# Whole float32 matmuls in the decode and the retention, instead of split fp32r parts

## The chip, the cores and the metric

The kernel runs on one core of one Trainium2 chip. The metric is device time in microseconds, as the median of the timed runs. The profile is of one execution. Engines are named as the profile names them: PE (TensorE's matmuls), PEld (its weight loads), DVE (VectorE), ACT (ScalarE), POOL (GpSimd) and SP (SyncE, whose queue issues every DMA here).

## What is computed

One step of a layer with three gated branches, for a prompt of 2048 tokens and for 8 sequences that are decoded, 16 new tokens each. One projection of the normed input feeds all branches; each branch's output is gated, projected, merged and projected again. Cut to the parts that the change touches:

```python
def fox_attend(q, c_q, q_pos, k, v, c_k):            # 8 heads x 64; decode: 16 queries, 2048 cached keys + 16 new
    s = einsum('bqhd,bkhd->bhqk', q, k) * 64 ** -0.5
    s = s + c_q[..., :, None] - c_k[..., None, :]    # cumulated log forget gates (axes moved)
    p = softmax(where(k_pos <= q_pos, s, -inf))
    return einsum('bhqk,bkhd->bqhd', p, v)

def retention_block(q, k, v, s, log_g):              # 4 heads, qk 128, v 256, state s 128 x 256
    inter = einsum('blhk,bhkv->blhv', q, s) * dec_q
    intra = einsum('bhlm,bmhv->blhv', einsum('blhk,bmhk->bhlm', q, k) * dmask, v)
    s_new = exp(log_g * L) * s + einsum('blhk,blhv,hl->bhkv', k, v, dec_k)
    return inter + intra, s_new

def memory_attend(q, mk, mv):                        # 4 heads x 128; decode: 16 queries, 256 cached memory tokens
    p = softmax(einsum('bthd,bmhd->bhtm', q, mk) * 128 ** -0.5)
    return einsum('bhtm,bmhd->bthd', p, mv)
```

## The kernel before

All multiplications keep close to float32 precision by splitting: a float32 operand x becomes a high part h (x cast to fp32r, on ACT) and a low part l = x - h (on DVE or POOL), and a product is three fp32r matmuls: h by h, h by l, l by h (`mm3` at L225, `mm3r` at L230; `split` at L200). The work runs in three stages.

The *projection* (to 1683 us) makes all of q, k, v and the gates and leaves them in DRAM; the FoX and memory queries and keys are stored there already split (qtH, qtL, ktH, ktL, mqH, mqL), the retention's q, k, v are stored whole.

Then *two lanes* are woven by hand-set costs (`weave`, L1007; the lanes at L1771 and L1792), so that the program order of their steps alternates; each engine then runs its own instructions in order. The right lane is the retention and then FoX's prompt attention. The left lane is the forget gates' sums, the prompt's memory attention (`mem_prompt`), the decode's memory attention (`decode_mem`), FoX's decode (`decode_fox`) and the first output block. The last stage is the other *output blocks*.

*Retention* (L1109). Sixteen units of 128 tokens and one for the 8 decoded sequences (`sample`), each started one step after the last. A unit loads q, k, v, transposes q and k (8 transposes), splits q (qh, ql), k (knh, knl) and v (vh, vl) in `ret_parts`, multiplies whole float32 scores of 128 columns in `ret_scores` (L1062) and splits the masked scores (smh, sml). Its outputs are 24 fp32r matmuls of 256 columns into `ry` (L1138) and its new state 12 into `rm` (L1146); the state is split for the next unit. Later steps normalise, gate, transpose and store (`ret_store`). `sample` runs sixteen steps, for each sequence and pair of heads: load a state, split it, mask query and key parts for the sequence (L1215, L1218), multiply 6 and 6 fp32r matmuls, add the decayed state and store it.

*FoX decode* (L1405). For each of 8 sequences: the queries of all heads stand as four 128 x 128 blocks (`qblk`), high and low. For each of four chunks of 512 cached keys, the keys come as rows (tile dkt), and for each group of 128 features four transposes (L1500) bring them to feature-major, `split` makes dkh and dkl, and `mm3r` multiplies 3 x 512 columns; a selector matmul (L1505) adds the forget sums. After the softmax the probabilities are transposed and split (dpr), the values (dvt) are split on POOL into dvh and dvl (L1542, L1543), and the values are multiplied as 64 fp32r matmuls of 256 columns (L1548): the stationary operand holds the high and the low probabilities of 64 rows side by side, and `sumid` adds the two halves at the end (L1564).

*Memory decode* (L1627) does the same with 256 memory tokens: 16 transposes (L1659), `split` into mkh and mkl, 12 matmuls of 256 columns, values cast and split (mvh, mvl), 4 matmuls of 512.

Of the kernel before, what the change touches and what calls it, by code (L numbers as in the profile page):

```python
# [72 lines left out]
def body(ctx: ExitStack, tc: tile.TileContext, a, o, stop=99):  # L73
# [106 lines left out]
    def f32(t):  # L180
        return t.bitcast(F32)
# [853 lines left out]
    def ret_parts(rw, q, k, v):  # L1035

        qt = rw.tile([P, 512], F32, name="qt")
        kt = rw.tile([P, 512], F32, name="kt")
        qh = rw.tile([P, 512], F32R, name="qh")
        ql = rw.tile([P, 512], F32R, name="ql")  # L1040
# [5 lines left out]
        S.copy(qh, qt)  # L1046
        G.tensor_tensor(ql, qt, f32(qh), ALU.subtract)
        knh = rw.tile([P, 512], F32R, name="knh")
        knl = rw.tile([P, 512], F32R, name="knl")
        S.copy(knh, k)  # L1050
        G.tensor_tensor(knl, k, f32(knh), ALU.subtract)
        vh = rw.tile([P, 1024], F32R, name="vh")
        vl = rw.tile([P, 1024], F32R, name="vl")
        S.copy(vh, v)
        G.tensor_tensor(vl, v, f32(vh), ALU.subtract)
        return qt, kt, qh, ql, knh, knl, vh, vl

    def ret_scores(rw, qt, kt, mask, nm="sm"):
# [4 lines left out]
        sm = rw.tile([P, 512], F32, name=nm, bufs=1)  # L1063
        V.tensor_tensor(sm, sc, mask, ALU.mult)
        smh = rw.tile([P, 512], F32R, name="smh")
        sml = rw.tile([P, 512], F32R, name="sml")
        S.copy(smh, sm)
        G.tensor_tensor(sml, sm, f32(smh), ALU.subtract)
        return smh, sml
# [21 lines left out]
    def ret_gate(rw, ob, i, sa, nb, g, nm="y"):  # L1091

        y = rw.tile([P, 1024], F32, name=nm)
# [15 lines left out]
    def retention(rp, rw):  # L1109
        NG, OB = 4, 5  # L1110
        cur = [None, None, None]
# [3 lines left out]
        def unit(t):  # L1115
# [3 lines left out]
            qt, kt, qh, ql, knh, knl, vh, vl = ret_parts(rw, q, k, v)  # L1119
            yield  # L1120
            smh, sml = ret_scores(rw, qt, kt, mask)
            yield
            so, soh, sol = cur
            ob = rw.tile([P, 4, 256], F32, name="ob", bufs=OB)
            for h2 in range(2):
                op = pry()

                prods = []
                for rnd in range(4):
                    for i in range(2):  # L1130
                        h = 2 * h2 + i
                        c = slice(h * P, (h + 1) * P)
# [725 lines left out]
```

## Time and profile before

| | us |
|---|---|
| median of the three timed runs | 3410.53 |
| fastest, slowest | 3404.25, 3414.77 |
| the profiled execution's own time | 3406.5 |
| its span, first to last instruction | 3404.7 |

| share of the span | PE | PEld | DVE | ACT | POOL |
|---|---|---|---|---|---|
| busy | 94% | 88% | 67% | 51% | 36% |

A matmul's record is longer than the time after which the next one starts, so a busy PE is not a full PE; the starts of matmuls in a row show what one costs. A group of instructions is named by its line, engine, operation and tiles (written <- read); its idle time is that of the engine just before the group's instructions, with what ended it. A stretch is a window of time from the span's start.

### The profile page before, as it was taken

To read this page: it belongs to the slowest core of one execution; us is meant where nothing else is said; L and a number is where in the kernel's file an instruction comes from. 1 tells how busy PE (TensorE), PEld (TensorE's weight loads), DVE (VectorE), ACT (ScalarE), POOL (GpSimd) and SP (SyncE) were. 2 spreads that over 40 slices of the span, in tenths; PEclk is the share of its full clock that TensorE was granted. 3 is DMA by queue.
4 is the path that set the end of the run, shared out by engine and by line. 5 is a ranking of instruction groups with operands and counts; after the bars stand their busy time and mean duration, and the time that the engine had idled before them with its cause. 6 is when DMAs were issued, how large, how long until landed. Compare 5 with 4: busy or idle time off the path is not lost. (4 is left out here: it accounts for less than half of the span.)

```text
span 3404.7 us, 60285 instructions
## 1 busy us (share of the span) xinstructions
PE 3195.5 (94%) x22299; PEld 2997.7 (88%) x22299; DVE 2271.3 (67%) x3732; ACT 1743.5 (51%) x3404; POOL 1217.7 (36%) x1122
## 2 busy tenths in 40 slices
PE   6999999999999999999878888999999988999999
PEld 5998999999999999999868766888887888888899
DVE  7677676665565666565588877887777886545444
ACT  4453444555344555445468755767776764223222
POOL 4436443110220010220176443777776764100000
PEclk8999999999999999999999987999999999999999
DMA  4776566567557667667567765455654457676665
GB/s 166 230 246 201 180 209 198 190 211 253 168 167 215 203 212 244 205 192 220 192 198 230 243 195 162 153 157 162 179 179 148 129 151 224 184 223 204 191 188 166
DMA packets 628219, 660.94 MB, mean 194 GB/s; under 512 B 46060, under 2 KB 549252, under 8 KB 627860
## 3 DMA queue, kind: packets, MB, share of 16 engines
q1 hardware_dynamic: 627924, 657.08, 62.5%
q8 instruction: 176, 2.88, 0.3%
q14 instruction: 119, 0.97, 0.1%
HBM read 477.52 MB, written 179.41 MB: 193 GB/s over the span
## 5 line engine op out<-in xcount | busy, mean ns | idle before, releaser
L400 DVE TENSOR_TENSOR wl<-wr,wh 128x1024 fp32r<-128x1024 f32 (+1 forms) x386 | 568.4, 1476 | 286.9 <-ACT wh L399 282.1
L399 ACT CAST wh<-wr 128x1024 fp32r<-128x1024 f32 (+1 forms) x386 | 404.6, 1050 | 309.9 <-PE b L451 128.0
L449 PE MATMUL a<-wh,ho 128*128 128x256 f32 (+1 forms) x1432 | 408.4, 286 | 18.1 <-ACT gz L707 11.3
L450 PE MATMUL a<-wl,ho 128*128 128x256 f32 (+1 forms) x1432 | 406.3, 284 | 5.8 <-DVE wl L400 5.8
L451 PE MATMUL a<-wh,ho 128*128 128x256 f32 (+1 forms) x1432 | 407.0, 284 | 1.0 <-DVE ho L276 1.0
L428 POOL TENSOR_TENSOR wr<-wr 128x1024 f32<-128x1024 f32 (+1 forms) x72 | 202.1, 2806 | 270.0 <-DMA wr<-in_w_in 235.0
L451 PE MATMUL b<-wh,ho 128*128 128x256 f32 (+1 forms) x1032 | 290.5, 282 | 5.4 <-DVE ho L276 5.4
L449 PE MATMUL b<-wh,ho 128*128 128x256 f32 (+1 forms) x1032 | 291.3, 283 | 4.0 <-ACT wh L399 2.3
L221 ACT CAST wh<-wraw 128x1024 fp32r<-128x1024 f32 x120 | 123.3, 1049 | 334.9 <-DMA wraw<-in_w_p 131.4
L449 PEld LDWEIGHTS a<-wh,ho 128*128 128x128 f32 x1432 | 273.4, 191 | 22.1 <-ACT gz L707 13.7
L450 PE MATMUL b<-wl,ho 128*128 128x256 f32 (+1 forms) x1032 | 290.4, 282 | 0.5 <-DVE wl L400 0.5
L450 PEld LDWEIGHTS a<-wl,ho 128*128 128x128 f32 x1432 | 273.7, 191 | 6.3 <-DVE wl L400 6.3
L451 PEld LDWEIGHTS a<-wh,ho 128*128 128x128 f32 x1432 | 273.7, 191 | 1.5 <-DVE ho L276 1.5
L449 PE MATMUL a<-ho,wh 128*128 128x384 f32 (+1 forms) x768 | 252.6, 329 | 1.6 <-ACT gz L707 1.6
L450 PE MATMUL a<-ho,wh 128*128 128x384 f32 (+1 forms) x768 | 252.9, 329 | 0.0
L451 PE MATMUL a<-ho,wl 128*128 128x384 f32 (+1 forms) x768 | 252.1, 329 | 0.0
L460 ACT COPY kp<-a 128x256 f32<-128x256 f32 (+3 forms) x384 | 153.3, 404 | 183.5 <-PE a L451 182.0
L1334 ACT ACTIVATE pt<-sc,f_mx 128x512 f32<-128x512 f32 (+2 forms) x320 | 201.5, 631 | 73.2 <-DVE f_mx L1333 48.4
L1338 POOL TENSOR_SCALAR pt<-pt,f_f,f_nm 128x512 f32<-128x512 f32 (+3 forms) x288 | 208.6, 740 | 82.2 <-DVE f_nm L1262 28.9
L1333 DVE TENSOR_REDUCE f_mx<-sc 128x1 f32<-128x512 f32 (+2 forms) x320 | 192.6, 604 | 39.4 <-PE sc L1327 21.7
L205 DVE TENSOR_TENSOR pl<-tp,ph 128x512 fp32r<-128x512 f32 (+2 forms) x352 | 193.5, 562 | 34.6 <-ACT ph L202 33.0
L1745 POOL TENSOR_TENSOR gm<-gm,gm 128x512 f32<-128x512 f32 (+2 forms) x40 | 45.6, 1139 | 447.4 <-DVE gm L1743 447.3
(437 smaller groups left out, 9901.0 us busy)
## 6 DMA issues: line engine op xcount, KB each, us to landing
wr<-in_w_in SPq DMA_DIRECT2D x170, 512.0 KB
wraw<-in_w_p SPq DMA_DIRECT2D x80, 512.0 KB
dkt<-in_cache_fox_k SPq DMA_DIRECT2D x64, 512.0 KB
dvt<-in_cache_fox_v SPq DMA_DIRECT2D x64, 512.0 KB
wr<-sum_gl SPq DMA_DIRECT2D x48, 512.0 KB
wraw<-in_w_out SPq DMA_DIRECT2D x40, 512.0 KB
gtd<-gz SPq DMA_DIRECT2D x96, 192.0 KB
gt<-gtd SPq DMA_DIRECT2D x24, 768.0 KB
```

Source lines behind the costliest of these rows:

```text
L205: V.tensor_tensor(l, src, f32(h), ALU.subtract)
L221: S.copy(whv[:, i * hc:(i + 1) * hc], rv)
L399: S.copy(h, t)
L400: eng.tensor_tensor(l, t, f32(h), ALU.subtract)
L428: G.tensor_tensor(out, x, y, op)
L449: T.matmul(out, lh(c), rh(c), start=first and c == 0, stop=False, skip_group_check=True)
L450: T.matmul(out, lh(c), rl(c), start=False, stop=False, skip_group_check=True)
L451: T.matmul(out, ll(c), rh(c), start=False, stop=last and c == 3, skip_group_check=True)
L460: S.copy(t[nm], t["a"])
L1333: V.tensor_reduce(nmx[:, j, ci:ci + 1], sc[:, :w], AX.X, ALU.max, negate=True)
L1334: S.activation(pt[:, :w], sc[:, :w], AF.Exp, bias=nmx[:, j, ci:ci + 1], accum_out=l[:, j, ci:ci + 1])
L1338: G.tensor_scalar(pt, pt, fb, 0.5 if r is None else r[:, j:j + 1], ALU.mult, ALU.mult)
```

## The change

The FoX decode, the memory decode and the retention multiply whole float32 operands, one float32 matmul for each three (or, for the decode's values, two half-wide pairs) of fp32r. The splits of q, k, v, scores, states, cached keys and cached values there go; the FoX and memory queries and new keys, which DRAM holds as two parts, are added together once (qw, kw). The cached keys of both attentions are handed to the kernel feature-major, so their transposes go as well. The masks of `sample` move from DVE to POOL, and the decay of the state goes into DVE's sum. The retention's order of state and output is swapped, and its tiles get more buffers. Nothing else is touched: FoX's prompt attention, the prompt's memory attention, the projection and the output blocks keep the split.

The diff, cut:

```diff
@@ ret_load, ret_turn (was ret_parts), ret_scores
-        q = rp.tile([P, 512], F32, name="rq")
-        k = rp.tile([P, 512], F32, name="rk")
-        v = rp.tile([P, 1024], F32, name="rv")
+        q = rp.tile([P, 512], F32, name="rq", bufs=2)
+        k = rp.tile([P, 512], F32, name="rk", bufs=4)
+        v = rp.tile([P, 1024], F32, name="rv", bufs=4)
...
-        S.copy(qh, qt)
-        G.tensor_tensor(ql, qt, f32(qh), ALU.subtract)
-        S.copy(knh, k)
-        G.tensor_tensor(knl, k, f32(knh), ALU.subtract)
-        S.copy(vh, v)
-        G.tensor_tensor(vl, v, f32(vh), ALU.subtract)
+        return qt, kt
...
-        S.copy(smh, sm)
-        G.tensor_tensor(sml, sm, f32(smh), ALU.subtract)
@@ retention, unit
-                for n, (dst, l, r) in enumerate(prods):
-                    T.matmul(dst, l, r, start=n == 0, stop=n == len(prods) - 1)
...
-                    mm3(up[:, (h % 2) * 256:(h % 2 + 1) * 256], knh[:, c], knl[:, c], vh[:, vc], vl[:, vc], True, True)
+                    T.matmul(up[:, i * 256:(i + 1) * 256], k[:, h * P:(h + 1) * P], v[:, h * 256:(h + 1) * 256], start=True, stop=True)
...
-                split(snh, snl, sn)
+                    T.matmul(op[:, i * 256:(i + 1) * 256], sm[:, h * P:(h + 1) * P], v[:, h * 256:(h + 1) * 256],
+                             start=i == 0, stop=t == 0 and i == 1)
+                        T.matmul(op[:, i * 256:(i + 1) * 256], qt[:, h * P:(h + 1) * P], so[:, h], start=False, stop=i == 1)
...
             y = ret_gate(rw, ob, j, *scales[t // NG], g)
             yield
+            yield
             ret_store(rw, y, t)
@@ retention, sample
-                    split(s0h, s0l, s0)
-                    G.tensor_tensor(s0, s0, gpb[:, hs], ALU.mult)
-                        V.tensor_copy(z[:, :, bs], f32(src).rearrange("p (h l) -> p h l", h=4)[:, hs, bs])
-                        V.tensor_scalar(z, f32(src)[:, h2 * 256:(h2 + 1) * 256], kc[:, K_BM + b:K_BM + b + 1], None, ALU.mult)
+                    G.tensor_copy(zb[:, :, bs], qt.rearrange("p (h l) -> p h l", h=4)[:, hs, bs])
+                    G.tensor_scalar(zk, k[:, h2 * 256:(h2 + 1) * 256], kc[:, K_BM + b:K_BM + b + 1], 1.0, ALU.mult, ALU.mult)
...
-                        mm3r(op[:, oc], zb[0][:, i], zb[1][:, i], s0h[:, i], s0l[:, i], False, b == NB - 1 and i == 1)
-                        mm3(up[:, oc], zk[:, 0, c], zk[:, 1, c], vh[:, vc], vl[:, vc], True, True)
-                    V.tensor_tensor(sn, up.rearrange("p (h v) -> p h v", h=2), s0, ALU.add)
+                        T.matmul(op[:, oc], zb[:, i], s0[:, i], start=False, stop=b == NB - 1 and i == 1)
+                        T.matmul(up[:, oc], zk[:, i * P:(i + 1) * P], v[:, h * 256:(h + 1) * 256], start=True, stop=True)
+                        V.scalar_tensor_tensor(sn[:, i], s0[:, i], kc[:, K_GP + 4 + h:K_GP + 5 + h], up[:, i * 256:(i + 1) * 256], ALU.mult, ALU.add)
@@ decode_fox
+        for w, (h, l) in ((qw, qs), (kw, ks)):
+            V.tensor_tensor(w, f32(h), f32(l), ALU.add)
...
-            kv = a["cache_fox_k"][b].rearrange("(p j) c -> p j c", p=P)
+            kv = a["cache_fox_k"][b].rearrange("g p k -> p g k")
...
-                        kt = dw.tile([P, 2, 512], F32, name="dkt", bufs=3)
-                        dma(kt, kv[:, 4 * ci + 2 * j:4 * ci + 2 * j + 2])
-                            T.transpose(p[:, j * P:(j + 1) * P], kts[j][:, g4 * P:(g4 + 1) * P], ident)
-                        split(kh, kl, p)
-                        mm3r(sc, qb[0][:, g4], qb[1][:, g4], kh, kl, g4 == 0, False)
+                        kt = dw.tile([P, 2, 512], F32, name="dkt", bufs=4)
+                        dma(kt, kv[:, 2 * g2:2 * g2 + 2, ci * 512:(ci + 1) * 512])
+                            T.matmul(sc, qb[:, 2 * g2 + g], kt[:, g], start=g2 == 0 and g == 0, stop=False)
...
-                split(prv[:, :, 0], prv[:, :, 1], p[:rows, :n * P].rearrange("p (a c) -> p a c", c=64))
+                S.copy(pr[:rows, :n], p[:rows, :n * P].rearrange("p (j c) -> p j c", c=P))
...
-                            vt = dw.tile([P, 2, 512], F32, name="dvt")
+                            vt = dw.tile([P, 2, 512], F32, name="dvt", bufs=4)
-                                G.tensor_scalar(vh[:, i], vt[:, i], 1.0, 1.0, ALU.mult, ALU.mult)
-                                G.tensor_tensor(vl[:, i], vt[:, i], f32(vh)[:, i], ALU.subtract)
-                                T.matmul(ov[:, c], lt, part[:, j % 2, c], start=ci == 0 and j == 0 and a2 == 0 and part is vh, stop=False)
+                        T.matmul(ov, pr[:, j], vt[:, j % 2], start=ci == 0 and j == 0, stop=False)
@@ decode_mem
-                        T.transpose(p[:, (2 * hh + m) * P:(2 * hh + m + 1) * P], kt[:, m, h * P:(h + 1) * P], ident)
-                split(kh, kl, p)
-                mm3r(sc[:64, :256], qb[0][:, h], qb[1][:, h], kh[:, c], kl[:, c], h == 0, h == 3)
+                T.matmul(sc[:64, :256], qb[:, h], kt[:, h], start=h == 0, stop=h == 3)
...
-                T.matmul(ov, lt, vh[:, m], start=m == 0, stop=False)
-                T.matmul(ov, lt, vl[:, m], start=False, stop=m == 1)
+                T.matmul(ov[:64], pr[:, m], vt[:, m], start=m == 0, stop=m == 1)
@@ _layout
+        "cache_fox_k": i["cache_fox_k"].reshape(NB, P, 16, 4, P).transpose(0, 3, 4, 2, 1).reshape(NB, 4, P, PAST), ...
+        "cache_mem_k": i["cache_mem_k"].reshape(NB, NMEM, 4, P).transpose(0, 2, 3, 1), ...
```

## Rows read from the trace of the kernel before

**Rows 1.** Windows by stage: us, busy time (instructions) of each engine, clock, DMA share.
```profile
1683.00:1757.00 74.00, 46.38 (x295) 39.58 (x294) 54.48 (x107) 40.36 (x76) 47.80 (x30) 0.82 0.69 209
1757.00:1902.00 145.00, 125.05 (x1000) 119.38 (x999) 122.26 (x282) 124.46 (x270) 98.68 (x86) 0.98 0.75 231
1902.00:2003.00 101.00, 83.50 (x588) 75.12 (x588) 84.70 (x233) 56.80 (x130) 47.61 (x64) 0.92 0.82 255
2003.00:2083.00 80.00, 54.54 (x255) 41.11 (x254) 50.55 (x158) 34.15 (x90) 29.69 (x42) 0.67 0.55 157
2083.00:2765.00 682.00, 652.86 (x4551) 563.17 (x4549) 535.63 (x1159) 475.67 (x1259) 492.87 (x648) 0.98 0.50 153
2765.00:3405.00 640.00, 617.00 (x3799) 557.84 (x3798) 350.37 (x485) 204.18 (x276) 99.98 (x81) 0.99 0.65 197
```

**Rows 2.** Timeline of PE: start us, us, line, tiles, shape, count; matmuls in a row.
```profile
1499.73 0.28 PE L449 MATMUL a<-wh,ho 128*128 128x256 f32 x1
...
1505.06 0.31 PE L449 MATMUL a<-ho,wh 128*128 128x320 f32 x1
...
2939.70 0.40 PE L226 MATMUL mr<-ih,wh 128*128 128x512 f32 x1
...
2945.79 0.39 PE L228 MATMUL mm<-ih,wl 128*128 128x512 f32 x1
...
2001.67 0.27 PE L1659 MATMUL tp<-kc,mkt 128*128 128x128 f32 x1
...
2007.89 1.04 PE L1659 MATMUL tp<-kc,mkt 128*128 128x128 f32 x8
...
1686.43 1.16 PE L1062 MATMUL rm<-qt,kt 128*128 128x128 f32 x8 [1.74 <-ACT kt L1045]
...
2223.79 1.00 PE L1564 MATMUL tp<-sumid,dos 128*128 128x64 f32 x8
```

**Rows 3.** Groups of PE by form, 2083 to 2765: count, busy, mean ns, idle before.
```profile
L1326 PE MATMUL sc<-ka,qa 128*128 128x512 f32 x195 | 88.3, 453 | 4.3 <-ACT pt L1334 4.1
...
L234 PE MATMUL ys<-dkl,qb 128*128 128x512 f32 x127 | 57.4, 452 | 7.3 <-DVE dkl L205 4.3 <-DVE f_nm L1257 3.0
L232 PE MATMUL ys<-dkh,qb 128*128 128x512 f32 x127 | 57.0, 449 | 4.6 <-ACT dkh L202 4.6
L1548 PE MATMUL ym<-dvh,dpr 128*128 128x256 f32 x256 | 52.4, 286 | 2.1 <-DVE dpr L205 2.1
```

**Rows 4.** Groups by form of ACT, POOL and DVE, 1683 to 2050, around the retention.
```profile
L1054 ACT CAST vh<-rv 128x1024 fp32r<-128x1024 f32 x17 | 18.0, 1059 | 9.2 <-DMA rv<-rvd 8.3 <-PE ry L1138 0.9
L202 ACT CAST sth<-st 128x1024 fp32r<-128x1024 f32 x15 | 16.0, 1065 | 7.4 <-DVE st L1152 7.4
...
L1055 POOL TENSOR_TENSOR vl<-rv,vh 128x1024 fp32r<-128x1024 f32 x17 | 44.8, 2635 | 25.7 <-ACT vh L1054 25.4
...
L1047 POOL TENSOR_TENSOR ql<-qt,qh 128x512 fp32r<-128x512 f32 x17 | 29.5, 1733 | 8.2 <-ACT qh L1046 5.0 <-issue 3.0 <-POOL vl L1055 0.2
...
L205 DVE TENSOR_TENSOR stl<-st,sth 128x1024 fp32r<-128x1024 f32 x15 | 23.5, 1566 | 0.6 <-ACT sth L202 0.6
...
L1218 DVE TENSOR_SCALAR kt<-knl,kc 128x256 fp32r<-128x256 f32 x16 | 10.3, 642 | 0.0
```

**Rows 5.** Groups by form of ACT, DVE and POOL, 2083 to 2765: the decode's splits.
```profile
L202 ACT CAST dkh<-tp 128x512 fp32r<-128x512 f32 x126 | 71.9, 589 | 62.1 <-PE tp L1500 60.0 <-PE ov L1380 0.7
...
L205 DVE TENSOR_TENSOR dkl<-tp,dkh 128x512 fp32r<-128x512 f32 x126 | 84.2, 685 | 43.0 <-ACT dkh L202 42.5
...
L1543 POOL TENSOR_TENSOR dvl<-dvt,dvh 128x512 fp32r<-128x512 f32 x124 | 156.8, 1285 | 0.5
```

**Rows 6.** Timeline of POOL and ACT, 1690 to 1760: start us, us, operation, idle before.
```profile
1710.52 5.41 POOL L1047 TENSOR_TENSOR ql<-qt,qh 128x512 fp32r<-128x512 f32 x1
...
1721.68 6.18 POOL L1055 TENSOR_TENSOR vl<-rv,vh 128x1024 fp32r<-128x1024 f32 x1
...
1732.59 0.59 ACT L1139 COPY ob<-ry 128x512 f32<-128x512 f32 x1 [8.54 <-PE ry L1138]
```

More of the change, by code (lines that the diff above doesn't have):

```diff
@@ L1153, in unit @@
                 else:
-                    S.copy(sn[:, hs], u)
+                    S.copy(sn[:, 2 * h2:2 * h2 + 2], u)
             if t == 15:
                 dma(o["ret_state_p"].rearrange("h k v -> k h v"), sn)
-            else:
-                snh = rw.tile([P, 4, 256], F32R, name="sth")
-                snl = rw.tile([P, 4, 256], F32R, name="stl")
-                split(snh, snl, sn)
-                cur[:] = [sn, snh, snl]
+            cur[0] = sn
+            for h2 in range(2):
+                op = pry()
+                for i in range(2):
+                    h = 2 * h2 + i
+                    T.matmul(op[:, i * 256:(i + 1) * 256], sm[:, h * P:(h + 1) * P], v[:, h * 256:(h + 1) * 256],
+                             start=i == 0, stop=t == 0 and i == 1)
+                if t:
+                    for i in range(2):
+                        h = 2 * h2 + i
+                        T.matmul(op[:, i * 256:(i + 1) * 256], qt[:, h * P:(h + 1) * P], so[:, h], start=False, stop=i == 1)
+                S.copy(ob[:, 2 * h2:2 * h2 + 2], op.rearrange("p (h v) -> p h v", h=2))
             j = t % NG
@@ L1509, in unit @@
                     for g4 in range(4):
[L1510 removed]
+                        T.matmul(sc[:, :16], qb[:, g4], kw[:, g4, bs], start=g4 == 0, stop=False)
                     T.matmul(sc[:, :16], selr[:16], cnT[:, bs], start=False, stop=False)
@@ L1551, in unit @@
                     dma(f32(vn), f32(vhl)[SEQ + b * TS:SEQ + (b + 1) * TS])
-                    for a2 in range(2):
-                        c = slice(a2 * 256, (a2 + 1) * 256)
-                        lt = pr[:16, 0, a2].rearrange("p r c -> p (r c)")
-                        T.matmul(ov[:, c], lt, vn[:, 4 * a2:4 * a2 + 4, 0:64], start=False, stop=False)
-                        T.matmul(ov[:, c], lt, vn[:, 4 * a2:4 * a2 + 4, 64:128], start=False, stop=a2 == 1)
+                    vw = dw.tile([16, 8, 64], F32, name="dvw", bufs=1)
+                    V.tensor_tensor(vw, f32(vn)[:, :, 0:64], f32(vn)[:, :, 64:128], ALU.add)
+                    T.matmul(ov, pr[:16, 0], vw.rearrange("p h d -> p (h d)"), start=False, stop=True)
                     os = dw.tile([P, 512], F32, name="dos", bufs=1)
@@ L1698, in unit @@
             for h in range(4):
-                T.matmul(p[:, h * 64:(h + 1) * 64], os[:, h * P:(h + 1) * P], sumid, start=True, stop=True)
+                T.transpose(p[:, h * 64:(h + 1) * 64], os[:, h * P:(h + 1) * P], ident[:64, :64])
             for h in range(4):
```

184 lines of the change are left out of this document (58 added, 126 removed).

## The prediction

> **What bounds the kernel now.** I read the stretches first [rows 1]: a table of five engines by stage. The projection ends at 1683 us and the last output blocks begin at about 2765; the diff touches neither. Between them lie four stretches: the start of the retention (1683 to 1757), its steady part beside the prompt's memory attention (to 1902), its sample beside the decode's memory attention (to 2003), a changeover (to 2083), and the long one (to 2765), the FoX prompt attention beside the FoX decode. The busy share of TensorE is a poor guide there, since a matmul's record reaches well past the start of the next. So I next took the time from start to start of matmuls that run back to back [rows 2]: 45 steps of 256 fp32r columns take 5.33 us, 0.118 each; 26 steps of 512 columns take 6.09, 0.234 each; eight transposes take 1.04 with 0.27 for the last, as a single one shows, so 0.11 each. A whole float32 matmul has two records: eight records of 128 columns take 1.16, so 0.126 a record, and eight of 64 columns take 1.00, so 0.104.
>
> With these steps I weigh each stretch. The steady part has 1000 records of forms that all lie near 0.117: 117 of 145 us, 81%. By the same count the start fills 35 of 74 (47%), the sample 70 of 101 (70%), the changeover 34 of 80 (43%, at a mean clock of 0.67 of full speed). In the long stretch 803 of 4551 records are 512 wide (195 of each score pass, 127 of each of the decode's three key passes, 32 selector rows [rows 3]): 188 us; the other 3748 at 0.113 in the mean are 423: 611 of 682, 90%. So TensorE bounds the long stretch, and the retention has several engines near the same level: in its steady part DVE is busy 84%, ACT 86%, POOL 68% and the DMA engines 75% [rows 1].
>
> **What the change does to TensorE.** No row shows a float32 matmul wider than 128 columns, and this price carries the sum. A 128-column record at 0.126 is longer than a 256-column fp32r matmul (0.118) and than the 64-column record (0.104), so it isn't the weight load that sets it; 0.126 fits two passes of 128 columns at the rate of fp32r. Taken on: two records of 0.234 for 256 columns (0.47), two of 0.47 for 512 (0.94). The ends: four times the 128-column matmul, 1.01; and, if the step from 64 to 128 columns (0.023) goes on as it is, 0.53. I take 0.94, nearest to the fp32r rows of the same widths.
>
> FoX decode, per batch row. Now: 64 key transposes (7.0), 48 score matmuls of 512 (11.2), 64 value matmuls of 256 (7.6), and 2.6 for new keys, new values and the final sums: 28.3. After: 16 scores of 512 (15.0), 16 values of 512 (15.0), and 2.6: 32.6. The difference of 4.3, eight times, is **+34 us of TensorE work** in the long stretch.
>
> Retention, per block of 128: 36 fp32r matmuls of 256 (4.25) become 12 float32 ones (5.6): +1.4, and +21 over 16 blocks. Sample: 192 and 12 fp32r matmuls (24.1) become 64 and 4 (32.0): +8. Memory decode: 16 transposes, 12 matmuls of 256, 4 of 512 and the sums (5.0) become 4 of 256, 2 of 512 and 4 transposes (4.2): -6 over eight rows. Together +23 up to 2083.
>
> **What it takes off the other engines.** In the retention the splits go [rows 4]: ACT loses vh and the state's cast (1.06 each) and three casts of half that width, some 4 us a block; POOL loses vl (2.64) and three like ql, 6.5 a block or more; DVE loses the state's low part, 1.6. In the sample POOL takes over DVE's masking of keys and queries: 256 and 32 columns a step, at most half and a sixteenth of ql's 1.7 us, about 1, and it loses the state's decay, 512 columns. In the long stretch ACT loses the key casts, DVE their low parts, POOL the values' low parts [rows 5], 72, 84 and 157 of 476, 536 and 493 us busy, and POOL the values' high parts too.
>
> *Start, 1683 to 1757: -10 (-18 to 0).* POOL's chain stands in the way here: one ql takes 5.41 us beside a mean of 1.73, one vl 6.18 beside 2.64, and ACT then sits idle 8.5 us before a copy of the output [rows 6]. All of that goes, and the loads of v no longer wait for vl to free one of two buffers. The forget gates' scan and the first landing of v stay, so I take about half of what is idle beyond them.
>
> *Steady part: -2 (-8 to +10).* 117 become 133 us of TensorE; the long stretch, whose other engines are busy 70 to 79%, reaches 90%, and here they fall to about 72% (DVE), 53% (ACT) and under 20% (POOL). At 92 to 93% it lasts 143. DMA then runs at 0.76, as now.
>
> *Sample: -10 (-20 to 0).* 70 become 74 us. DVE loses some 33 of its 85 us: in each of 16 steps two key masks (0.64) and the low part of half a state (half of 1.57) [rows 4]. What ends last then is the DMA: 0.82 of 101 us is 83 [rows 1]; I let it be 0.91 busy, so 91 us.
>
> *Changeover: -3 (-10 to +5).* Its chain, the sample's statistics and output, then FoX's first short blocks, is not edited; the memory decode beside it gets lighter, two sums of 512 columns (query and key parts) come in on DVE and two memsets of 640 go.
>
> *Long stretch: +15 (-5 to +35).* 611 + 34 = 645 us. Of the 71 us unfilled now, 14 are idle times that the change removes: before dkh, dkl and dpr [rows 3]. Scores and values then read what a DMA has brought, with four buffers each, and their long matmuls leave FoX's chain more time. So 682 + 34 - 14 and some 5 less from freer engines: 697, a fill of 92.5%.
>
> *Keys feature-major: 0.* The count and size of the loads stay (64 of 512 KB by the code); the contiguous piece falls from 4 to 2 KB for FoX and from 2 to 1 KB for memory. DMA is 0.50 busy in the long stretch; the keys are a third of its bytes, so even twice the time per byte gives 0.67, still hidden. If the four buffers didn't cover a late load, TensorE would wait and everything queued behind it on that engine, FoX's scores among it; that cost, up to 20, is in the range. The values' buffers grow from two to four, and nothing new waits on SP's queue.
>
> Sum against the profiled execution's 3406.5: -10 - 2 - 10 - 3 + 15 = -10, 3396.5. That execution lies 4 below the median of the three timed runs, so the forecast is **3400 us**.
>
> **The rivals.** *TensorE pays in full (slower).* Place: the long stretch and the steady retention. If the 10% unfilled there come from FoX's own chain and from issue, not from the splits, the fill stays at 90% and 81 to 85%: 645/0.90 is 717 (+35), the steady part 157 (+12), less 20 from start, sample and changeover: +27, 3437. It decides once the long stretch's fill stays under 91%. For it: only 14 us of named waits are the decode's. Against: nothing else is then near full.
>
> *The work is absorbed (faster).* The fill of the long stretch rises to 94.5%, so it stays at 682 (0); the retention, freed of all but DMA, goes 45 us faster: 3365. For it: the 26 steps of the output blocks stand without a gap [rows 2], so TensorE can be filled. Against: DMA, 243 us of work in the three stretches [rows 1], would be 0.88 busy over 275. Beside this rival stands a rule: the Trainium skill, "Perfetto Trace Analysis", Identifying the Most-Contended Engine, says that TensorE's headroom is judged by the busy share of weight loads, not of matmuls. The long stretch shows 563 of 682 us, 83%; by it there would be 119 us of room and the 34 would vanish, 3385 with my other terms.
>
> *Whole float32 isn't that dear.* At 0.53 for 512 columns the decode's row costs 19 instead of 28, and the long stretch loses 80 us: about 3300. Only the fit of one width speaks against it. The Trainium skill, "FP8 and Floating Point Precision", TensorE Precision Notes, gives four passes for true FP32, which would leave my price at 0.94.
>
> **How the numbers follow.** Forecast 40%, paid in full 30%, absorbed 20%, cheap float32 4%, and 6% for late loads or a longer changeover (3440 to 3470). The range runs from 3360, the absorbed case, to 3440, the paid one. About 0.3% (10 us) can be told from no change. The forecast sits on that edge: of its 40, 20 are faster, 18 the same, 2 slower; of the paid case 24 slower and 6 the same; with the rest, faster 44%, same 24%, slower 32%. Without the cases on the other side, the forecast's own range is 3385 to 3418.
>
> **What would show it.** Starts of the decode's float32 score matmuls 0.47 apart per record (0.94 a pair); the retention ending near 1980 instead of 2003; the long stretch at about 697 us, with fewer waits of TensorE on ACT and DVE; the part after FoX unchanged at 640. The prediction is wrong if the pair is far from 0.94, if TensorE waits on loads of dkt or dvt, if FoX's own chain (pl, pt) leaves as much idle as now, or if the retention's steps stay at 12 us.

## The result, and the profile after

The changed kernel takes 3380.3 us (median of four executions, 3372.1 to 3382.9) where the kernel before takes 3409.4: a ratio of 0.991, 95% interval 0.989 to 0.993, so 29 us shorter. The forecast was 3400. Its profiled execution took 3379.1 us with a span of 3377.4, against 3406.5 and 3404.7 before, so the two traces differ by 27.3.

The page after, first part (busy time of each engine, share, instructions):

```profile
PE 3215.3 (95%) x20971; PEld 2885.5 (85%) x20971; DVE 2057.2 (61%) x3446; ACT 1599.3 (47%) x3153; POOL 828.0 (25%) x789
```

POOL lost 390 us of work, DVE 214, ACT 144; TensorE has 20 us more. To see where the time went, I take four events that both programs have. First the kernel before, grouped timelines of the tiles rm, dkt and doT; the range behind each group is its first and last start, in us: the masked scores (the last is the sample's, issued as the prompt's blocks end), the sample's new states, the first operation on a cached FoX key, and the decode's outputs.

```profile
L1064 DVE TENSOR_TENSOR sm<-rm,rmask x17: 653/675/692, 1694.1 to 1902.7; 128x512 f32<-128x512 f32 x17
...
L1228 DVE TENSOR_TENSOR y<-rm,st x16: 649/678/692, 1916.6 to 2002.2; 128x512 f32<-128x512 f32 x16
...
L1500 PE MATMUL tp<-kc,dkt x512: 270/272/476, 2078.5 to 2680.4; 128*128 128x128 f32 x171
...
L1569 DVE TENSOR_TENSOR doT<-tp,dfg x16: 204/222/228, 2224.8 to 2760.3; 64x64 f32<-64x64 f32 x16
```

The same in the changed kernel (the first operation on a key is now a score matmul):

```profile
L1052 DVE TENSOR_TENSOR sm<-rm,rmask x17: 646/674/692, 1695.2 to 1879.4; 128x512 f32<-128x512 f32 x17
...
L1192 DVE SCALAR_TENSOR_TENSOR sn<-st,kc,rm x32: 464/475/481, 1880.3 to 1930.1; 128x256 f32<-128x256 f32 x32
...
L1460 PE MATMUL ys<-dkt,qb x256: 590/592/1223, 2024.9 to 2620.3; 128*128 128x512 f32 x128
...
L1512 DVE TENSOR_TENSOR doT<-tp,dfg x16: 203/218/228, 2184.6 to 2726.5; 64x64 f32<-64x64 f32 x16
```

| between these events | before | after | difference | predicted |
|---|---|---|---|---|
| up to the last masked scores (start and steady part) | 1902.7 | 1879.4 | -23.3 | -12 |
| sample | 99.5 | 50.7 | -48.8 | -10 |
| changeover, to the first key operation | 76.3 | 94.8 | +18.5 | -3 |
| long stretch, to the last output of the decode | 681.8 | 701.6 | +19.8 | +15 |
| the rest | 644.4 | 650.9 | +6.5 | 0 |
| sum | 3404.7 | 3377.4 | -27.3 | -10 |

The first row can be divided: the fifth of the masked scores, some 60 us into the retention, and the twelve steps behind it (timelines of DVE, before and after; then TensorE's window behind it, after):

```profile
1757.87 0.69 DVE L1064 TENSOR_TENSOR sm<-rm,rmask 128x512 f32<-128x512 f32 x1 [0.27 <-PE rm L1062]
...
1754.37 0.69 DVE L1052 TENSOR_TENSOR sm<-rm,rmask 128x512 f32<-128x512 f32 x1 [0.98 <-PE rm L1050]
```

```profile
1754.00:1879.00 125.00, 125.00 (x840) 117.16 (x840) 91.08 (x265) 78.38 (x189) 18.78 (x38) 1.00 0.76 235
```

So the start is only 3.5 us shorter, and the twelve steps take 125 us in place of 145. TensorE was busy 125 of those 145 us before [rows 1] and is busy for the whole 125 now. By the prices further down and those of [rows 2], 288 records of 256 float32 columns, 96 of 128, 240 transposes and 216 fp32r matmuls make some 126 us: the steady part is now as long as TensorE's work.

Windows of the changed kernel, cut at its own events (us; busy time and instructions of PE, PEld, DVE, ACT, POOL; granted clock, DMA share, GB/s), to be held against [rows 1]:

```profile
1743.00:1879.00 136.00, 132.60 (x880) 123.75 (x879) 98.91 (x278) 88.35 (x214) 21.58 (x44) 0.97 0.76 235
1879.00:1930.00 51.00, 49.95 (x311) 45.42 (x309) 36.04 (x91) 27.80 (x74) 20.66 (x60) 1.00 0.97 308
1930.00:1990.00 60.00, 41.94 (x171) 23.37 (x170) 17.03 (x71) 14.21 (x37) 2.49 (x10) 0.80 0.90 245
1990.00:2025.00 35.00, 29.69 (x123) 17.03 (x121) 20.45 (x64) 19.62 (x61) 10.11 (x18) 0.84 0.56 159
2025.00:2727.00 702.00, 676.43 (x3610) 475.39 (x3611) 418.80 (x1036) 412.44 (x1129) 260.61 (x389) 0.97 0.51 151
```

The sample is half as long, and its DMA engines are now full (0.97 at 308 GB/s). TensorE is nearly full too: busy 50 of the 51 us, some 50 by the count of steps, with 1 us of waits, so which of the two bounds it isn't settled. Behind it TensorE is busy 42 of 60 us at a clock of 0.80. The timeline of PE shows what stands there, the memory decode, waiting for its keys (in brackets the idle time before, and what ended it):

```profile
1947.38 6.26 PE L1598 MATMUL ys<-mkt,mq 128*64 128x256 f32 x16 [7.46 <-DMA mkt<-in_cache_mem_k]
...
1962.00 5.33 PE L1598 MATMUL ys<-mkt,mq 128*64 128x256 f32 x16 [2.77 <-DMA mkt<-in_cache_mem_k]
...
1977.08 5.08 PE L1598 MATMUL ys<-mkt,mq 128*64 128x256 f32 x16 [4.11 <-DMA mkt<-in_cache_mem_k]
```

Before, its key transposes ran from 1965 to 2009, beside the sample's last third; after, its score matmuls run from 1947 to 1990, beginning when the sample has ended. So sample and memory decode belong together: from the last masked scores to the memory decode's last key operation it was 106.0 us before and is 110.6 after. The bytes say the same: the sample's window moved 101 x 255 = 25.8 MB before [rows 1] and moves 51 x 308 = 15.7 MB now. Of the difference, 7.9 MB are the memory decode's keys and values: 15 of its 16 loads of 512 KB were issued in the first window, none in the second.

The price of a float32 matmul can be read from runs of equal ones (timeline of PE, start and length of the run, in us; two records make one matmul):

```profile
1917.65 0.38 PE L1189 MATMUL rm<-rv,kz 128*128 128x256 f32 x1
1928.22 1.03 PE L1189 MATMUL rm<-rv,kz 128*128 128x256 f32 x4
...
2344.23 3.60 PE L1494 MATMUL ym<-dvt,dpr 128*128 128x512 f32 x8
...
2619.90 1.02 PE L1460 MATMUL ys<-dkt,qb 128*128 128x512 f32 x2
```

A run lasts one record and the steps between starts. For 256 columns that is (1.03 - 0.38) / 3 = 0.217 a record; for 512, from the runs of eight and of two, (3.60 - 1.02) / 6 = 0.43. So a matmul of 512 columns costs 0.86, where I took 0.94, and one of 256 costs 0.43, where I took 0.47.

### The profile page after: what moved, and what is told of

The parts are those of the page before. It is cut to its first block, busy times and chain, and to the rows that moved or that the text cites. A ratio compares the mean times of both kernels' runs of the same rounds, so it can differ in the third digit from the quotient of the medians.

```text
span 3377.4 us, 56780 instructions
## 1 busy us (share of the span) xinstructions
PE 3215.3 (95%) x20971; PEld 2885.5 (85%) x20971; DVE 2057.2 (61%) x3446; ACT 1599.3 (47%) x3153; POOL 828.0 (25%) x789
## 5 line engine op out<-in xcount | busy, mean ns | idle before, releaser
L1297 DVE TENSOR_REDUCE f_mx<-sc 128x1 f32<-128x512 f32 (+2 forms) x320 | 192.3, 605 | 97.5 <-PE sc L1293 50.7
L202 ACT CAST ph<-tp 128x512 fp32r<-128x512 f32 (+2 forms) x352 | 167.5, 490 | 111.4 <-PE tp L1324 93.4
```

The source lines that it names most:

```text
L202: S.copy(h, src)
L1297: V.tensor_reduce(nmx[:, j, ci:ci + 1], sc[:, :w], AX.X, ALU.max, negate=True)
```

## The experiments

The theory: the gain is the retention's, whose splits stood in the way of its matmuls; part of it is given back because the memory decode and its loads, which lay beside the sample, now lie behind it; the FoX decode costs a little. The rivals: the gain comes from the decodes or from the layout of the keys; the buffers make it; TensorE's work alone sets the long stretch. All differences "against the kernel before" are between medians of executions taken together; their intervals are some 4 to 11 us to either side, so a difference between two such differences is uncertain by some 9 to 14.

**One part at a time.** Three kernels take one part of the change each into the kernel before: the retention's functions; `decode_fox` with its keys' layout; `decode_mem` with its keys' layout. One line of each, in this order:

```diff
-                    mm3(up[:, (h % 2) * 256:(h % 2 + 1) * 256], knh[:, c], knl[:, c], vh[:, vc], vl[:, vc], True, True)
+                    T.matmul(up[:, i * 256:(i + 1) * 256], k[:, h * P:(h + 1) * P], v[:, h * 256:(h + 1) * 256], start=True, stop=True)
...
-                        mm3r(sc, qb[0][:, g4], qb[1][:, g4], kh, kl, g4 == 0, False)
+                            T.matmul(sc, qb[:, 2 * g2 + g], kt[:, g], start=g2 == 0 and g == 0, stop=False)
...
-                mm3r(sc[:64, :256], qb[0][:, h], qb[1][:, h], kh[:, c], kl[:, c], h == 0, h == 3)
+                T.matmul(sc[:64, :256], qb[:, h], kt[:, h], start=h == 0, stop=h == 3)
```

> The kernel before, with the retention alone in whole float32 (prompt and sample); both decodes stay split and their keys token-major. Theory (the gain is the retention's, because the splits leave ACT, POOL and DVE; the long stretch gives part of it back): the sample ends near 1930 us as in the kernel changed, the FoX decode starts near 2025 to 2045, and the long stretch keeps its 688 us; the whole is 35 to 50 us shorter than before, more than the full change's 27. Rival (the gain is the decodes', which lose 64 key transposes a row and all their splits): 0 to 10 us shorter.

> The kernel before, with the FoX decode alone in whole float32 and its cached keys feature-major; retention and memory decode as before. Theory: the long stretch grows from 688 to some 705 us and nothing else moves: 10 to 20 us longer than before. Rival (the decode is lighter without transposes and splits): 10 to 25 us shorter. If only the float32 work counted, at 0.86 us for 512 columns: 8 x 1.7 = 13 us of work, over a fill of 90% 15 us longer.

> The kernel before, with the memory decode alone in whole float32 and its cached keys feature-major. Theory: it stands beside the retention's sample, which is the longer; 0 to 5 us shorter than before, or up to 5 longer if the 1 KB pieces of its keys slow the loads beside those of the states. Rival (the memory decode is what ends last in the changeover): 10 to 20 us shorter.

Measured against the kernel before: the retention alone 39 us shorter (ratio 0.989, 0.987 to 0.991), more than the whole change; the FoX decode alone 4 longer (1.0014, 1.0001 to 1.0028); the memory decode alone 11 shorter (0.997, 0.995 to 0.999). So the gain is the retention's: its sample ends at 1927.1 us (the sample's new states, retention alone), and its long stretch keeps 684 us. The decodes' rival falls as an account of the whole.

```profile
L1192 DVE SCALAR_TENSOR_TENSOR sn<-st,kc,rm x32: 464/475/481, 1877.2 to 1927.1; 128x256 f32<-128x256 f32 x32
```

With the FoX decode alone the long stretch did grow, from 681.8 to 697.7 us, but most of that is a shifted border. The first keys need no transposes now, and TensorE multiplies them ahead of the gates' sums, so they begin 54.7 us after the sample's last state, not 76.3 (timeline of PE, FoX decode alone):

```profile
2058.54 6.70 PE L1496 MATMUL ys<-dkt,qb 128*128 128x512 f32 x8 [2.25 <-POOL qb L1468]
...
2067.52 0.43 PE L1432 MATMUL tp<-ctot,sufm 128*128 128x64 f32 x2 [1.35 <-DVE ctot L1425]
```

The three parts alone add up to 46 shorter, 17 more than the change gives, little more than the intervals leave open. The memory decode's 11 have the size that the rival there gave (10 to 20), and are not explained: its executions lay between 3389.6 and 3410.3, and the profiled one was the longest. In its trace the first FoX key comes 64 us after the sample's last state and not 76, as the rival would have it, but FoX's last maximum only 2 us earlier than before.

**The memory decode behind the sample.** Two runs on the changed kernel: one edits the left lane's costs, which say how far it is issued beside the retention, the other the length of the pieces in which the memory keys are loaded (the keys are handed over to match).

```diff
-                    yield from paced(mem_prompt(*pools(s2, "left", ("dp", 1), ("dw", 2))), 35, 160)
+                    yield from paced(mem_prompt(*pools(s2, "left", ("dp", 1), ("dw", 2))), 35, 110)
...
-                    yield from paced(decode_mem(*pools(s2, "left", ("dp", 1), ("dw", 2))), 13, 100)
+                    yield from paced(decode_mem(*pools(s2, "left", ("dp", 1), ("dw", 2))), 13, 150)
```

```diff
-            dma(kt, a["cache_mem_k"][b].rearrange("h p m -> p h m"))
+            dma(kt, a["cache_mem_k"][b].rearrange("p (h m) -> p h m", h=4))
```

> The changed kernel, with two costs of the left lane changed: the prompt's memory attention 110 in place of 160, the memory decode 150 in place of 100 (their sum stays). So the prompt's memory attention is issued faster beside the retention, and the memory decode begins beside the retention's last blocks and its sample, not behind them. Theory (the retention's 73 us shrink to 30 because the memory decode, which stood beside the sample before, now stands alone behind it and waits for its loads): the FoX prompt attention's last block ends 15 to 35 us earlier than in the changed kernel, and the whole is 15 to 35 us shorter. Rival (sample and memory decode are bound together by DMA, 30 MB in 111 us, wherever they stand): the sample gets longer by what the changeover loses, 0 to 5 us shorter. Second rival (the start of FoX's prompt attention is a chain of its own, and the memory decode fills its gaps for nothing now): 0 to 10 us longer.

> The changed kernel, with the memory keys handed over with a feature's four heads side by side, so that each partition's load is one run of 4 KB instead of four of 1 KB; bytes and order of loads are the same. Theory: the waits of TensorE on mkt (14 us in the changed kernel) come from where the loads are issued and from the other loads and stores in flight, not from the pieces: 0 to 3 us shorter. Rival (the 1 KB pieces are slow): the memory decode shrinks from 43 to some 30 us, 8 to 15 us shorter.

With the earlier memory decode 48 us shorter than before, so 19 more than the change; with the longer pieces 31, so 2 more, which is nothing. The pieces are not the cause: with the longer ones TensorE's wait for the memory keys falls from 14.3 to 6.7 us in the trace, but the memory decode still takes 41 us. What counts is the place of the memory decode, its loads with it: issued earlier, it has 0.8 us of that wait. The windows of the run with the earlier memory decode (up to the last masked scores, to the memory decode's last keys, to the first FoX key):

```profile
1743.00:1894.00 151.00, 147.73 (x1011) 137.45 (x1010) 113.74 (x328) 100.26 (x254) 27.18 (x58) 1.00 0.76 234
1894.00:1970.00 76.00, 68.79 (x328) 48.17 (x326) 36.27 (x120) 25.73 (x60) 15.08 (x52) 0.96 1.00 318
1970.00:2003.00 33.00, 26.09 (x130) 15.19 (x129) 18.24 (x62) 18.67 (x55) 6.50 (x13) 1.00 0.85 232
```

The blocks end 15 us later, but sample and memory decode together take 75 us in place of 111, with the DMA engines full at 318 GB/s and TensorE's clock at 0.96 in place of 0.80 in the gap. The rival that DMA binds them wherever they stand falls too, since what came earlier went beside the blocks.

**What of the splits slowed the retention.** Three runs on the changed kernel: the splits' work beside the float32 matmuls, read by nobody; the same work in the path; and the buffers few again, without that work. The first two call a helper for q, k, v and the scores (on ACT and POOL) and for the states (on ACT and DVE); in the second the matmuls read what it returns, and its buffers are those of the third, but for the sample's states, which keep three.

```diff
+    def idle_split(rw, eng, src, n):
+        if eng == "ACT" and 1:
+            S.copy(rw.tile([P, 1024], F32R, name="ja", bufs=1)[:, :n], src)
...
+        if eng == "POOL" and 1:
+            G.tensor_tensor(rw.tile([P, 1024], F32R, name="jp", bufs=1)[:, :n], src, src, ALU.subtract)
```

```diff
+    def through(rw, src, n, name, eng):
+        x1 = rw.tile([P, n], F32, name=name + "1", bufs=1)
+        x2 = rw.tile([P, n], F32, name=name + "2")
+        S.activation(x1, src, AF.Copy, scale=0.0)
+        eng.tensor_tensor(x2, src, x1, ALU.subtract)
+        return x2
```

```diff
-        v = rp.tile([P, 1024], F32, name="rv", bufs=4)
+        v = rp.tile([P, 1024], F32, name="rv", bufs=2)
...
-                    s0 = rw.tile([P, 2, 256], F32, name="st0", bufs=3)
+                    s0 = rw.tile([P, 2, 256], F32, name="st0")
```

> The changed kernel with the work of the retention's splits put back beside it: the same casts on ACT (q, k, v, scores, state), subtractions on POOL and DVE, and two key masks of 256 columns a sample step on DVE, all into scratch that nobody reads. The float32 matmuls and the buffers stay. If the splits cost throughput (an engine is full with them): the sample ends 40 to 70 us later, near 1970 to 2000, and the whole is 20 to 38 us longer than the changed kernel. If they cost latency (matmuls wait for cast and subtraction): the sample ends within 15 us of 1930, and the whole is 0 to 8 us longer.

> The changed kernel with the same work in the path: the retention's q, k, v, scores and states go through an operation of ACT and then one of POOL (states: DVE) before the float32 matmuls read them, as the low parts did, with buffers as few as before; values are unchanged by it. The masks of the sample are on DVE as before. If latency or throughput of the splits made the retention slow: the sample ends near 1990 to 2005 and the whole is 30 to 45 us longer than the changed kernel, as the kernel before or some 5 more. If what counts is that three fp32r matmuls became one float32 one: 0 to 10 us longer.

> The changed kernel with the retention's tiles in two buffers again: k, v (four), the transposed q, the gated output and the sample's states (three). Theory (the splits are what counts): 0 to 8 us longer than the changed kernel. Rival (the deeper buffers let loads run ahead, and that is the gain): 20 to 40 us longer, with the sample at 80 us or more.

With the splits in the path the kernel is back where it was: 2 us longer than before (1.001, 0.9998 to 1.0022). The fair neighbour is the run with as few buffers, which is 42 us shorter than before (0.988, 0.985 to 0.991). Between these two lie 44 us for the splits' work in the path, with the same float32 matmuls and the same order of state and output, so that order alone isn't the gain. Beside it, read by nobody, the work costs 20 (9 us shorter than before, against 29), though its readers also hold the tiles that they read. Neither expectation for that run holds whole: the sample ends at 1944 us, within 15 of 1930, but the time is 20 longer. In its trace the blocks are 4 us longer and the sample 10, of which 5 are given back by FoX's end; the other 9 of the trace's 18 us lie after FoX, where nothing is edited. Its window of the blocks, with ACT at least as busy as before:

```profile
1743.00:1884.00 141.00, 133.93 (x878) 123.40 (x878) 121.62 (x297) 127.95 (x275) 91.91 (x92) 0.98 0.73 224
```

So the work costs by filling engines, and more than twice as much where the matmuls have to wait for it. In the path (window of the blocks, then TensorE's longest waits from 1690 to the blocks' end: total, times, longest):

```profile
1743.00:1911.00 168.00, 149.24 (x920) 135.18 (x921) 135.65 (x322) 130.84 (x286) 104.26 (x94) 0.93 0.64 198
```

```profile
PE rm L1122 <- POOL tv L1050: 10.2, 2, 9.5
PE tp L1566 <- DVE m_ot L1575: 9.5, 4, 3.4
PE ry L1137 <- POOL ts L1050: 5.2, 2, 3.5
```

One wait for POOL's share of v is 9.5 us; that is the start's chain of [rows 6]. The splits' 44 us lie in the prompt's blocks (the last masked scores at 1910.6 against 1872.0); the sample differs by 4 only (63.9 and 59.9). It ends at 1974.5, before the 1990 to 2005 that was expected.

```profile
L1059 DVE TENSOR_TENSOR sm<-rm,rmask x17: 646/679/692, 1692.6 to 1910.6; 128x512 f32<-128x512 f32 x17
...
L1052 DVE TENSOR_TENSOR sm<-rm,rmask x17: 653/659/692, 1693.2 to 1872.0; 128x512 f32<-128x512 f32 x17
```

The named waits don't add up to the 44: those for the splits' results are 15 us, all but 2 of them before the fifth masked scores. 22 us come in the twelve steps behind it, where TensorE waits longest for the prompt's memory attention (m_ot, on DVE); in which way the splits slow those steps isn't shown.

That the fewer buffers are 12 us shorter than the changed kernel I had not expected. It is close to the noise: the executions lie from 3363.0 to 3376.6 and from 3372.1 to 3382.9, and their means differ by 11, give or take 10. In the traces the deeper buffers cost time at the start, where the fifth masked scores come at 1754.4 and with two buffers at 1740.9; half of that is given back in the steps behind it, so the blocks end 7 us earlier with two. The sample is then 9 us longer, at a DMA share of 0.87 and not 0.97, and the memory decode takes 28 us and not 43, with no wait for its keys (tile mkt, the run with fewer buffers: the score matmuls' range, the loads' issues, and the only long wait, 9.0 us of it PE's and the rest PEld's):

```profile
L1598 PE MATMUL ys<-mkt,mq x64: 378/379/689, 1946.0 to 1974.1; 128*64 128x256 f32 x64
L184 SPq DMA_DIRECT2D mkt<-in_cache_mem_k x8: 367/368/469, 1939.4 to 1967.7; - x8
its engine sat idle before it (us, times) until:
  POOL mq L1593: 18.2, 2
```

Loads that run further ahead fit this, but which of the five tiles it is wasn't tried. For the memory decode it isn't the states' buffers alone: the run with the splits in the path keeps three of them, and its memory decode takes 28 us too (1986.7 to 2014.8).

**What sets the long stretch.** Three runs on the changed kernel: the decode's values split as before (their parts on POOL); keys, queries, values and probabilities all split as before, keys still feature-major; and keys token-major, transposed on chip, but multiplied whole.

```diff
-                        T.matmul(ov, pr[:, j], vt[:, j % 2], start=ci == 0 and j == 0, stop=False)
+                        for part in (vh, vl):
+                            for a2 in range(2):
...
+                                T.matmul(ov[:, c], lt, part[:, j % 2, c], start=ci == 0 and j == 0 and a2 == 0 and part is vh, stop=False)
```

```diff
-                            T.matmul(sc, qb[:, 2 * g2 + g], kt[:, g], start=g2 == 0 and g == 0, stop=False)
...
+                            split(kh, kl, kt[:, g])
+                            mm3r(sc, qb[0][:, 2 * g2 + g], qb[1][:, 2 * g2 + g], kh, kl, g2 == 0 and g == 0, False)
```

```diff
-                            T.matmul(sc, qb[:, 2 * g2 + g], kt[:, g], start=g2 == 0 and g == 0, stop=False)
...
+                            T.transpose(p[:, j * P:(j + 1) * P], kts[j][:, g4 * P:(g4 + 1) * P], ident)
...
+                        S.copy(kf, p)
+                        T.matmul(sc, qb[:, g4], kf, start=g4 == 0, stop=False)
```

> The changed kernel, with the values and the probabilities of the FoX decode split again, as before (high and low parts of the values on POOL, 64 fp32r matmuls of 256 columns a row in place of 16 float32 ones of 512); its keys stay whole and feature-major. TensorE's work falls by 8 x 16 x (0.86 - 4 x 0.118) = 50 us, POOL's rises by some 330. Theory (TensorE's work bounds the long stretch): 30 to 50 us shorter than the kernel changed. Rival (the stretch waits for FoX's own chain through ACT and DVE, and TensorE's work fits into it): 0 to 10 us shorter. Second rival (POOL's splits come late again and hold the value matmuls up): no change or up to 15 us longer.

> The changed kernel, with keys, queries, values and probabilities of the FoX decode all split as before, but with feature-major keys, so without transposes. TensorE per row: 48 key matmuls of 512 columns (11.2 us) and 64 value matmuls of 256 (7.6) and 2.6, 21.4 in place of about 32; 80 us less in eight rows. ACT gets its 72 us of key casts back, DVE its 84 us of low parts, POOL some 330 us. Theory by the run with the values split (21 us for 50 us of TensorE work): 30 to 35 us shorter than the changed kernel. If TensorE's work alone set it: 80 shorter. Rival (the splits come late and lengthen FoX's chain through ACT and DVE): no shorter than with the values alone split, some 20 us shorter than the changed kernel, or less.

> The changed kernel, but the FoX keys lie token-major again and are transposed on TensorE (64 transposes a row, 0.11 us each, and a copy by ACT for each four); they are multiplied whole. 56 us more of TensorE work, and some 70 us more of ACT. Theory (the layout is what pays for the float32 matmuls: the work counts, and little of it finds room): 40 to 60 us longer than the changed kernel. Rival (the long stretch has room, as the float32 work alone cost 5 us for 13): 0 to 20 us longer.

Against the kernel before: values split 49 us shorter (20 more than the change), everything split 25 shorter (4 less than the change, nothing that can be told), token-major 1 shorter (28 less). The profiled execution with the values split was the fastest of its four, 13 us under their median, so its trace shows 33 us where the medians show some 20. In the second expectation the changed row was summed as 32 us; with the prices above it is 32 x 0.86 + 2.6 = 30.1, so the work falls by 70 us, not 80. The windows of the long stretch, in this order:

```profile
2014.00:2695.00 681.00, 636.41 (x3888) 498.87 (x3889) 481.94 (x1074) 416.46 (x1134) 495.53 (x647) 0.95 0.52 156
```

```profile
2026.00:2730.00 704.00, 642.80 (x4062) 542.33 (x4063) 582.00 (x1207) 483.95 (x1268) 543.53 (x663) 0.92 0.50 151
```

```profile
2045.00:2757.00 712.00, 704.96 (x4086) 510.79 (x4086) 412.04 (x989) 472.97 (x1248) 257.98 (x380) 0.99 0.48 143
```

Each line can be taken apart into time in which TensorE was not busy, time lost to the granted clock (one less the mean clock, times the length; to some 4 us, by its two digits), and the rest. Against it stands the change in TensorE's work as counted from records.

| kernel | length | not busy | lost to the clock | rest | rest against the changed kernel | by records |
|---|---|---|---|---|---|---|
| before (2078 to 2760) | 682 | 29 | 14 | 639 | -16 | -15 |
| changed | 702 | 26 | 21 | 655 | | |
| values split | 681 | 45 | 34 | 602 | -53 | -50 |
| all split | 704 | 61 | 56 | 586 | -69 | -70 |
| keys token-major | 712 | 7 | 7 | 698 | +43 | +56 |

The rest follows the records, to 3 us where the splits come back and 13 short for token-major keys; the length doesn't. But the two losses overlap where the clock is low while TensorE stands idle: with each stretch cut into 180 windows, some 8 of the 56 us fall on idle time with everything split, 4 of the 34 with the values split and 2 or less in the others, so the rest for everything split is nearer -59. Of 70 us taken off TensorE with everything split, 35 came back as idle time, then, and 25 to 35 as a lower clock. TensorE's longest waits are for FoX's own chain, and they are as long with the values alone split (two lines each, everything split, then values split):

```profile
PE sc L1290 <- ACT pt L1298: 15.8, 29, 1.5
PE ov L1344 <- DVE pl L205: 11.1, 6, 3.6
...
PE sc L1290 <- ACT pt L1298: 16.0, 24, 3.5
PE ov L1344 <- DVE pl L205: 11.2, 8, 4.3
```

The keys' split adds shorter waits to them, the longest for its own low parts (dkl, 5.1 us). So neither "TensorE's work alone" nor "the stretch has room" holds: work that is added finds part of its place in idle time and in the clock, and work that is taken off leaves part of itself there. The values' split pays: POOL has the time (496 of 681 us), and 16 float32 matmuls of 0.86 become 64 of 0.118. The keys' split on top of it doesn't: it puts 100 us on DVE and 68 on ACT, and 16 us more of idle time and some 17 to 22 more lost to the clock take back its 20 us and more; that the load on ACT and DVE is the reason is argued, not shown.

**Both that helped.** The values split and the memory decode earlier, in one kernel.

> The changed kernel with both edits that shortened it: the values of the FoX decode split again (21 us shorter alone) and the memory decode issued earlier (20 us shorter alone). Theory: they touch different stretches (2025 to 2726 and 1883 to 2025) and add up: 36 to 44 us shorter than the changed kernel, some 3340 us. Rival (FoX's own chain from its first block to its last is one chain, and an earlier start only adds waits to it): 20 to 28 us shorter, no better than either alone.

3348.1 us (3344.1 to 3359.4), 60 shorter than before (0.983, 0.980 to 0.986), 31 less than the changed kernel: it beats both kernels, and lies between the two expectations, which the intervals don't tell apart (some 11 to 13 us to either side of the 31). The last maximum of a FoX block starts 36 us earlier than in the changed kernel, where the two runs alone had 32 and 20; but the 32 are from the fastest of four executions. Whether the gains add up in full stays open.

## Why the prediction was right, and where it was wrong

The sign held, the time lies in the range, and the forecast was 20 us too long. That it came so near is in part luck: the sample was missed by 39 us one way and the changeover by 21 the other. By its steps:

- *The price.* 0.94 was mis-sized: 0.86. The Trainium skill, "FP8 and Floating Point Precision", TensorE Precision Notes, gives four passes for true FP32; as an estimate from that, a pass of 512 columns takes 0.86 / 4 = 0.215 us, 2.38 columns a ns, near the upper clock level of 2.4 GHz. My fit took its pass from fp32r, whose 0.234 [rows 2] is 9% longer. The decode's added work is 15 us, not 34.
- *Start and steady part, -12.* It was -23. That the splits stand in the way was right (44 us, the run in the path against the run with fewer buffers), but I put the gain in the wrong place. The start, which I gave 10 us for POOL's chain, is 3.5 shorter; the steady part, which I gave 2, is 20. The step that failed there is the fill: I let TensorE stop at 92 to 93%, and it is full.
- *Sample, -10.* It was -49. The step that failed is the DMA floor: I took the 83 us of DMA time in its window for the sample's own, when 10 of the 25.8 MB left the window, 7.9 of them the memory decode's. The 51 us aren't a DMA floor of the sample's own either: the states, in and out, are 28 loads and stores of 256 KB, 7.3 of the window's 15.7 MB, and TensorE has some 50 us of work there.
- *Changeover, -3.* It was +18, the other half of the same mistake: what leaves the sample's window comes up behind it. Sample and memory decode as one went from 106.0 to 110.6 us, where I had both ending sooner. What is left of the gain there is that FoX's first blocks now begin 58 us before the memory decode's last keys, not 2.
- *Long stretch, +15.* +20 in the trace, so right in size, but by other terms: 16 of work, 3 less idle, 7 more lost to the clock, where I had 34 of work and 19 less idle. Of the 14 us that I read from [rows 3] as the decode's waits, 3.0 are ended by f_nm, a part of FoX's softmax, so 11 were. These went as told, but the sign of being wrong that I had named is there: FoX's own chain (pt and pl) leaves 14.5 us idle, 9.8 before. The wait for pt grew from 4.6 to 14.1 (TensorE's waits, before, 2083 to 2765, then the changed kernel, 2025 to 2727: total, times, longest):

```profile
PE ov L1380 <- DVE pl L205: 5.2, 7, 2.4
PE sc L1326 <- ACT pt L1334: 4.6, 8, 1.6
...
PE sc L1290 <- ACT pt L1298: 14.1, 27, 1.6
PE tp L1396 <- DVE ctot L1389: 2.5, 1, 2.5
...
PE ov L1344 <- DVE pl L205: 0.4, 1, 0.4
```

  And as a cost of the change it is less: the FoX decode alone made the kernel 4 us longer (0 to 10), as its keys begin 20 us earlier.
- *Keys feature-major, 0.* The long stretch shows no wait of TensorE for dkt or dvt, and the memory keys in longer pieces gave 2 us, within what can't be told from none. As predicted. What the layout saves is the transposes: kept, they cost 28 us, so it is the layout that pays for the FoX decode's float32 matmuls.
- *After FoX, unchanged.* From the last maximum of FoX to the end 584.0 us before and 587.5 after; over the profiled runs 584 to 596 with nothing edited there, so differences below some 10 us between two traces aren't read from that part.

Of the rivals, *paid in full* had its condition met: by the prediction's count the long stretch holds 611 + 15 = 626 us of steps in 702, 89%, under its 91. But 15 us of work don't cost what 34 would, and the retention gave more. *Absorbed* was right for the retention and wrong for the long stretch. The rule cited there, the Trainium skill's "Perfetto Trace Analysis", Identifying the Most-Contended Engine, names the share of peak FLOPs beside that of weight loads. By weight loads alone it would now see still more room, since they fell from 83% to 68% of the stretch; the run with 56 us of transposes added, and some 60 us of copies on ACT, took 28 us longer, so half of the transposes found none. The measurement decides. *Cheap float32* is refuted by the 0.86; by its own prices it would have saved 70 us, not 80 (8 rows of 8.7).

## What to carry to other kernels

Before a DMA floor is taken from a window, ask whose bytes are in it: a faster stage pushes its neighbour's loads out of the window, and they wait behind it; issuing that neighbour earlier gave 19 us more. Where several engines are near full, replacing three cheap matmuls with one dear one pays if it takes work out of the matmuls' path, until TensorE is full, as it is now beside the retention; the choice is to be made operand by operand, by the engine that does the split: float32 for the retention, a split on an idle POOL for the values. More buffers are an edit of their own, to be measured alone.

## What the hardware showed that I had not expected

- A float32 matmul of 512 columns steps by 0.86 us, less than four times the 0.234 of an fp32r matmul of the same width.
- Of some 70 us of work taken off TensorE in the long stretch with everything split, 35 came back as idle time and 25 to 35 as a lower granted clock: 0.97 in the changed kernel, 0.95 with the values split, 0.92 with everything split.
- Two buffers in place of three and four in the retention made the kernel 12 us shorter, give or take 10.
